# Two of the modulation sections made in each attention are summed by VectorE in two staging tiles, the rest stay matmuls

## The chip, the cores and the metric

The kernel runs on one core of a Trainium2 chip. The metric is the device time of one execution in microseconds (us), here the median of three runs. The engines are TensorE (PE, with its weight loads PEld), VectorE (DVE), ScalarE (ACT), GpSimd (POOL) and SyncE (SP), which issues nearly all DMAs.

## The reference

The program is one inference step of a two-layer backbone. It handles 640 tokens of width 1024: 128 context tokens and 512 latent tokens, two groups that share the weights but not the conditioning vector. Each layer is

```
mod = silu(cond) @ w_mod + b_mod            # 1024 x 9216, split into 9 sections of 1024
sh1, sc1, g1, sh2, sc2, g2, sh3, sc3, g3 = split(mod, 9)
x = LN(alpha*x + 0.5*g1*SwiGLU_1(x*(1+sc1)+sh1))
x = LN(alpha*x + g2*W_out[RG-LRU | GQA | MLA](x*(1+sc2)+sh2))
x = LN(alpha*x + 0.5*g3*SwiGLU_2(x*(1+sc3)+sh3))
```

All is float32. A modulation section (layer, s) is two vectors of 1024 (one for each group's cond), each a product of a vector of 1024 with a 1024x1024 block of `w_mod`, 4 MB. There are 18 sections, numbered s = 0 to 8 in each layer; s = 2, 5 and 8 are gates.

## The kernel before

The big products are split: a float32 weight comes by DMA into a staging tile ("raw", a ring of `NR` = 7 tiles of 128x1024 floats, counted by `raw_out`), ACT rounds it to a high part, DVE subtracts to get the low part, and PE makes three products. The program is a list of steps, each with loads, splits and a body that yields; `run` walks through them, `feed` issues the next loads of one common queue whenever `raw_out` is below `NR`, and `tick` advances background generators once at every yield. A tile scheduler then orders each engine's instructions; nothing in the parts spoken of here is ordered by hand. An instruction can be issued earlier than where it is traced, if its inputs are ready.

A modulation section is eight steps (`mod_steps`), one for each 128 rows of its block of `w_mod`, and can be made in two ways. In `body` a step is four matmuls of 256 columns with `cst`, the two conds as 32 columns of weights, in four column groups of PE (L364); they sum in one bank of the tag `p1`, of which there are two. In `vbody`, used in the FFN stages (`late == "v"`), a step is four DVE operations of 128x512: for each group's cond and each half, raw times one column of `cst` plus the sum so far (L331; the first step has no sum, L329). The two sums are tiles of 128x1024. After the eighth step, eight matmuls with `sel` add up the 128 partitions (L340). Both ways end in `mod_end`: bias, and then a small transpose or a gate's trip through DRAM.

`PLAN` says which sections are made where. In the mixer of layer 0 ("m0") five are made, in that of layer 1 ("m1") three, all with `body`, during the attention. The attention of the latent tokens (`att_sample`) goes through 48 units, one for each pair of a head (8 GQA, then 4 MLA) and a block of 128 queries. A unit is: scores on PE (L1751), the maximum on DVE (L1765) and a tiny product (L1766), the exponent on ACT (L1767), a reciprocal on DVE (L1775), the normalisation on POOL (L1776), five transposes on PE two units later (L1785), their copy on ACT (L1790), and values on PE (L1713), five for each four units. `att_sample` yields twice for each unit, and `env["unit"]` counts units as their scores are traced. Beside it `side` makes the context tokens' attention and MLA's projections.

`mod_fill` is the generator that places the modulation: groups of `MODG` = 4 steps, group i not before unit `MOD0 + i*MODN//len(msteps)` (i counts steps), which is 6, 9, 13, ... 40 in layer 0 and 6, 12, 18, 25, 31, 37 in layer 1, and not before all four raw tiles are traced. The step that starts it, `attend_mods`, comes behind the last projection (`tokens(768, ...)`), which already runs beside the first units. Its loads stand in the queue behind the weights of MLA and ahead of those of `W_out`.

Of the kernel before, what the change touches and what calls it, by code (L numbers as in the profile page):

```python
# [18 lines left out]
P = 128  # L19
D = 1024  # L20
# [18 lines left out]
NB = 23  # L39
LAG = 2  # L40
AVN = (0, 0, 5, 0)
MOD0, MODN, MODG = 6, 38, 4
YK, YQ0, YQ1, YC, YR, YM = 5, 1, 0, 0, 2, 2
NORM_ACT = 256, 512
EVAC = 2, 1
# [15 lines left out]
GROUPS = (1, slice(0, 128)), (0, slice(128, 640))  # L61
PLAN = {
    "f00": [[], [], [(0, 2), (0, 3), (0, 4)]],
    "m0": [[], [(0, 5), (0, 6), (0, 7), (0, 8), (1, 0)]],
    "f01": [[], [], [(1, 1), (1, 2)]],
    "f10": [[], [], [(1, 3), (1, 4)]],
    "m1": [[], [(1, 5), (1, 6), (1, 7)]],
    "f11": [[], [], [(1, 8)]],
}
LN_LAG = 1, 1  # L70
# [39 lines left out]
class Kern:  # L110
# [194 lines left out]
    def mod_steps(self, l, s, late=False):  # L305

        nc, I = self.nc, self.I
        st = {}
        steps = []
        for k in range(KT):  # L310
            hold = {}

            def load(k=k, hold=hold):
                t = self.raw([P, D])
                nc.sync.dma_start(out=t, in_=I["w_mod"][l, k * P : (k + 1) * P, s * D : (s + 1) * D])
                hold["raw"] = t

            def vbody(k=k, hold=hold):

                if k == 0:  # L320
                    st["acc"] = [self.X([P, D]) for _ in range(2)]
                    st["bm"] = bias_rows()
                for g in range(2):
                    acc, c = st["acc"][g], self.cst[:, k, g : g + 1]
                    for h in range(2):
                        cs = slice(h * 512, (h + 1) * 512)
                        e = nc.gpsimd if (g, h) in VP else nc.vector
                        if k == 0:
                            e.tensor_scalar(acc[:, cs], hold["raw"][:, cs], c, 1.0, op0=ALU.mult, op1=ALU.mult)  # L329
                        else:  # L330
                            e.scalar_tensor_tensor(  # L331
                                acc[:, cs], hold["raw"][:, cs], c, acc[:, cs], op0=ALU.mult, op1=ALU.add
                            )
                        yield
                self.raw_out -= 1
                if k == KT - 1:
                    st["ps"] = self.p1()
                    for g in range(2):
                        for c in range(4):
                            nc.tensor.matmul(  # L340
                                st["ps"][32 * c : 32 * c + 32, 0:256],
                                lhsT=self.sel[:, g],
                                rhs=st["acc"][g][:, c * 256 : (c + 1) * 256],
                                start=(g == 0),
                                stop=(g == 1),
                                skip_group_check=True,
                                tile_position=(0, 32 * c),
                            )
                    self.mod_end(l, s, st)

            def bias_rows():
                bm = self.bm[self.bm_i]
                self.bm_i ^= 1
                src = I["b_mod"][l, s * D : (s + 1) * D].rearrange("(c n) -> c n", c=4)
                for g in range(2):
                    nc.sync.dma_start(out=bm[g : 97 + g : 32, :], in_=src)
                return bm

            def body(k=k, hold=hold):
                if k == 0:  # L360
                    st["ps"] = self.p1() if late else self.p2()[:, 0, :]
                    st["bm"] = bias_rows()
                for c in range(4):
                    nc.tensor.matmul(  # L364
                        st["ps"][32 * c : 32 * c + 32, 0:256],
                        lhsT=self.cst[:, k, :],
                        rhs=hold["raw"][:, c * 256 : (c + 1) * 256],
                        start=(k == 0),
                        stop=(k == KT - 1),
                        skip_group_check=True,  # L370
                        tile_position=(0, 32 * c),
                    )
                self.raw_out -= 1
                if k == KT - 1:
                    self.mod_end(l, s, st)
                yield

            steps.append(Step([load], [], vbody if late == "v" else body))
            steps[-1].ready = lambda hold=hold: "raw" in hold
        return steps  # L380

# [770 lines left out]
    def mixer_steps(self, l, mods):  # L1152
        nc, I, O = self.nc, self.I, self.O
        env = {}
# [421 lines left out]
        def mla_weights():  # L1576

            h = [{}, {}]

            def load0():  # L1580
                t = self.raw([P, 2, 384])
                w = I["mla_w_uq"][l]
                nc.sync.dma_start(out=t[:, 0], in_=w[0:128])
                for d in range(2):
                    nc.sync.dma_start(out=t[64 * d : 64 * d + 64, 1], in_=w[128:192])
                h[0]["raw"] = t

            def load1():
                t = self.raw([P, 512])
                nc.sync.dma_start(out=t[:, 0:256], in_=I["mla_w_uk"][l])  # L1590
                nc.sync.dma_start(out=t[:, 256:512], in_=I["mla_w_uv"][l])
                h[1]["raw"] = t

            def sp(i, key, shape):
                def go():
                    env[key] = split(h[i]["raw"], shape)
                    self.raw_out -= 1

                go.ready = lambda: "raw" in h[i]
                return go  # L1600

            def body():
                yield

            return Step([load0, load1], [sp(0, "uq", [P, 2, 384]), sp(1, "ukv", [P, 512])], body)
# [287 lines left out]
        S = []  # L1893

        def proj(c0, post, first=None):
            h = {}
            ld, sp = self.weight(I["w_in"][l][:, c0 : c0 + P].rearrange("(k p) f -> p k f", p=P), [P, KT, P], h, self.W)
            n = len(S)

            def body():  # L1900
                h["ps"] = self.p2("pg" if n % 2 == 0 else "pu")
                for c in range(2):
                    yield from self.mtile(h["ps"], h, c)
                post(h["ps"])
                yield

            return h, ld, sp, body

        def bgpost(gen):
            def post(ps):  # L1910
                self.bg.append(gen(ps))

            return post

        h0, l0, s0, _ = proj(0, None)
        h1, l1, s1, _ = proj(256, None)
# [14 lines left out]
            yield  # L1931

        S.append(Step([l0, l1], s0 + s1, first))
        for ls in mods[0]:
            S += self.mod_steps(*ls, late=True)
        keep = {}

        def xa1(ps):
# [90 lines left out]
        for c0, post in ((128, xa1), (384, ga1)):  # L2029
            h, ld, sp, body = proj(c0, post)  # L2030
# [3 lines left out]
        h, ld, sp, body = proj(1504, bgpost(c_post))  # L2034
# [38 lines left out]
            self.drain()  # L2073

        S.append(mla_weights())
        msteps = [st for ls in mods[1] for st in self.mod_steps(*ls, late=True)]

        def mod_fill():

            for i in range(0, len(msteps), MODG):  # L2080
                part = msteps[i : i + MODG]
                while env.get("unit", 0) < MOD0 + i * MODN // len(msteps) or not all(st.ready() for st in part):
                    yield
                for st in part:
                    for _ in st.body():
                        pass
                yield

        def attend_mods():
            self.bg.append(mod_fill())  # L2090
            yield from attend()
# [364 lines left out]
```

## Time and profile before

| | |
|---|---|
| median of 3 runs | 2520.85 us (2518.51 to 2522.15) |
| the profiled execution | 2519.84 us, of which the span from first to last instruction is 2518.0 us |
| PE, PEld busy | 2418.0 us (96%), 2186.4 us (87%) |
| DVE busy | 1934.2 us (77%) |
| ACT, POOL busy | 1135.9 us (45%), 347.0 us (14%) |

Busy is the share of the span in which an engine has at least one instruction under way. Register, branch and DMA-issuing instructions don't count. The first and the second attention lie at about 608 to 767 us and 1849 to 2000 us of the span. Unit numbers here count from 0, by the reductions of L1765.

### The profile page before, as it was taken

How to read it: one execution, taken by the hardware profiler on the slowest of the kernel's cores; microseconds unless marked ns; L12 is line 12 of the kernel's file. 1: busy time of each engine (PE TensorE's matmuls, PEld its weight loads, DVE VectorE, ACT ScalarE, POOL GpSimd, SP SyncE). 2: the span in 40 equal slices, each digit the busy share in tenths (PEclk: the TensorE clock that was granted, in tenths of full speed). 3: DMA queues.
4: the chain of work that ended last, by engine and by line, in shares of the span. 5: the costliest groups of instructions: out<-in, count | busy, mean ns of one | idle time of the engine just before them, and what ended most of it. 6: DMA issues, size and time to landing. Idle time of an engine off the chain costs nothing. (4 is left out here: it accounts for less than half of the span.)

```text
span 2518.0 us, 40146 instructions
## 1 busy us (share of the span) xinstructions
PE 2418.0 (96%) x15732; PEld 2186.4 (87%) x15732; DVE 1934.2 (77%) x3333; ACT 1135.9 (45%) x2062; POOL 347.0 (14%) x347
## 2 busy tenths in 40 slices
PE   8899999998999999999999999999999999999997
PEld 7898998898769999999889989988976799999986
DVE  5898977878555988876799878778785479777777
ACT  3443343565662543333355333435656534443332
POOL 2100002026322000000100000021363210000022
PEclk9999999999999999999999999999999999999999
DMA  8344433232562343432424333242223423333331
GB/s 283 108 147 142 152 118 109 79 105 65 176 219 85 105 139 118 131 112 84 126 68 149 120 124 116 89 123 87 80 96 123 132 76 102 115 103 105 114 93 51
DMA packets 273270, 293.80 MB, mean 117 GB/s; under 512 B 13645, under 2 KB 224185, under 8 KB 273081
## 3 DMA queue, kind: packets, MB, share of 16 engines
q1 hardware_dynamic: 273080, 291.23, 37.0%
q8 instruction: 124, 2.03, 0.3%
q14 instruction: 66, 0.53, 0.1%
HBM read 270.79 MB, written 18.83 MB: 115 GB/s over the span
## 5 line engine op out<-in xcount | busy, mean ns | idle before, releaser
L930 PE MATMUL pb<-u,w 128*128 128x320 f32 x3600 | 554.6, 309 | 2.2 <-DVE b L976 2.2
L930 PEld LDWEIGHTS pb<-u,w 128*128 128x128 f32 x3600 | 534.8, 188 | 7.0 <-issue 4.6
L930 PE MATMUL pb<-s,w 128*128 128x320 f32 x2700 | 424.4, 310 | 2.0 <-DVE w L906 0.9
L902 ACT CAST w<-raw 128x512 fp32r<-128x512 f32 x525 | 315.9, 619 | 230.6 <-DVE raw L898 151.6
L930 PEld LDWEIGHTS pb<-s,w 128*128 128x128 f32 x2700 | 402.4, 188 | 7.1 <-DVE w L906 1.8
L906 DVE TENSOR_TENSOR w<-raw,w 128x512 fp32r<-128x512 f32 x525 | 357.0, 692 | 45.8 <-ACT w L902 44.4
L1042 PE MATMUL p<-dw,b 128*128 128x512 f32 x830 | 330.3, 398 | 18.8 <-DVE x L1055 16.7
L1043 PE MATMUL p<-dw,b 128*128 128x512 f32 x830 | 324.5, 391 | 0.0
L1044 PE MATMUL p<-dw,b 128*128 128x512 f32 x830 | 324.2, 391 | 0.0
L194 ACT CAST dw<-raw 128x1024 fp32r<-128x1024 f32 x86 | 87.9, 1051 | 367.7 <-PE p L1043 331.0
L1042 PEld LDWEIGHTS p<-dw,b 128*128 128x128 f32 x830 | 156.1, 188 | 68.4 <-DVE x L1055 34.5
L1055 DVE TENSOR_TENSOR x<-x,p 128x512 f32<-128x512 f32 x200 | 136.5, 682 | 86.2 <-PE p L1044 85.6
L1044 PEld LDWEIGHTS p<-dw,b 128*128 128x128 f32 x830 | 156.2, 188 | 33.3
L1043 PEld LDWEIGHTS p<-dw,b 128*128 128x128 f32 x830 | 156.3, 188 | 29.2
L331 DVE SCALAR_TENSOR_TENSOR x<-raw,cst,x 128x512 f32<-128x512 f32 x224 | 163.6, 751 | 19.5 <-DMA raw<-in_w_mod 19.5
L526 PE MATMUL p<-u,w 128*128 128x320 f32 (+2 forms) x528 | 167.1, 318 | 7.4 <-ACT u L517 7.4
L1004 POOL TENSOR_SCALAR x<-x 128x1024 f32<-128x1024 f32 x8 | 9.5, 1184 | 1151.0 <-DMA x<-gd 500.0
L527 PE MATMUL p<-u,w 128*128 128x320 f32 (+2 forms) x528 | 166.4, 317 | 1.5 <-DVE u L518 1.4
L528 PE MATMUL p<-u,w 128*128 128x320 f32 (+2 forms) x528 | 164.8, 314 | 0.0
L199 DVE TENSOR_TENSOR dw<-raw,dw 128x1024 fp32r<-128x1024 f32 x86 | 105.3, 1228 | 41.9 <-ACT dw L194 41.7
L1765 DVE TENSOR_REDUCE sm<-p 128x1 f32<-128x640 f32 x96 | 78.8, 822 | 42.3 <-PE p L1751 37.6
L898 DVE TENSOR_TENSOR raw<-raw,raw 128x512 f32<-128x512 f32 x150 | 103.0, 687 | 10.6 <-DMA raw<-in_ffn_w_up 8.7
(363 smaller groups left out, 4436.1 us busy)
## 6 DMA issues: line engine op xcount, KB each, us to landing
raw<-in_w_mod SPq DMA_DIRECT2D x132, 512.0 KB
raw<-in_ffn_w_gate SPq DMA_DIRECT2D x88, 512.0 KB
raw<-in_ffn_w_up SPq DMA_DIRECT2D x88, 512.0 KB
raw<-in_ffn_w_down SPq DMA_DIRECT2D x88, 512.0 KB
xd<-x SPq DMA_DIRECT2D x30, 512.0 KB
raw<-in_w_in SPq DMA_DIRECT2D x26, 512.0 KB
t<-xd SPq DMA_DIRECT2D x40, 256.0 KB
raw<-in_w_out SPq DMA_DIRECT2D x16, 512.0 KB
```

What stands on the lines that cost most here:

```text
L199: nc.vector.tensor_sub(l, hold["raw"], f(hold["hi"]))
L331: e.scalar_tensor_tensor(acc[:, cs], hold["raw"][:, cs], c, acc[:, cs], op0=ALU.mult, op1=ALU.add)
L526: nc.tensor.matmul(out, lhsT=wh, rhs=xh, start=start, stop=False)
L527: nc.tensor.matmul(out, lhsT=wh, rhs=xl, start=False, stop=False)
L528: nc.tensor.matmul(out, lhsT=wl, rhs=xh, start=False, stop=stop)
L902: nc.scalar.copy(w[:, 0], at(src))
L906: nc.vector.tensor_sub(w[:, 1], at(src), f(w[:, 0]))
L930: nc.tensor.matmul(out, lhsT=a1, rhs=b1, start=(start and k == 0 and i == 0), stop=(k == 3 and i == 2), skip_group_check=not start,)
L1042: nc.tensor.matmul(pt, lhsT=hh[:, ts], rhs=d["hi"][:, cs], start=(i == 0), stop=False)
L1043: nc.tensor.matmul(pt, lhsT=hh[:, ts], rhs=d["lo"][:, cs], start=False, stop=False)
L1044: nc.tensor.matmul(pt, lhsT=hl[:, ts], rhs=d["hi"][:, cs], start=False, stop=(i == len(ms) - 1))
L1055: nc.vector.tensor_add(x[:, cs], x[:, cs], pt)
```

## The change

In each mixer the first two sections of the list, (0,5) and (0,6) in layer 0, (1,5) and (1,6) in layer 1, are made by `vbody`, now also for `late == "ring"`. Their sums are not tiles of the pool `X` but two tiles of the raw ring: two entries `room` ahead of a section's first load take them, and `raw_out -= 2` gives them back at its end. The other sections (three in layer 0, one in layer 1) stay with `body` in groups of four. `mod_fill` goes by a list of turns: vector step i not before unit `3 + i*22//16`, groups of four PE steps not before units 25, 28, 31, 35, 38 and 41 in layer 0 and 25 and 35 in layer 1. A vector step yields after its second and fourth operation and once more, so it takes three ticks, one unit and a half.

```
-MOD0, MODN, MODG = 6, 38, 4
+V0, VN, P0, PN = 3, 22, 25, 20
...
-    "m0": [[], [(0, 5), (0, 6), (0, 7), (0, 8), (1, 0)]],
+    "m0": [[(0, 5), (0, 6)], [(0, 7), (0, 8), (1, 0)]],
...
-    "m1": [[], [(1, 5), (1, 6), (1, 7)]],
+    "m1": [[(1, 5), (1, 6)], [(1, 7)]],
...
-                    st["acc"] = [self.X([P, D]) for _ in range(2)]
+                    if late == "v":
+                        st["acc"] = [self.X([P, D]) for _ in range(2)]
...
+                    if late == "ring":
+                        self.raw_out -= 2
                     self.mod_end(l, s, st)
...
-            steps.append(Step([load], [], vbody if late == "v" else body))
+            def room():
+
+                st.setdefault("acc", []).append(self.raw([P, D]))
+
+            lds = [room, room, load] if late == "ring" and k == 0 else [load]
+            steps.append(Step(lds, [], vbody if late in ("v", "ring") else body))
...
-        for ls in mods[0]:
-            S += self.mod_steps(*ls, late=True)
...
-        msteps = [st for ls in mods[1] for st in self.mod_steps(*ls, late=True)]
+
+        vsteps = [st for ls in mods[0] for st in self.mod_steps(*ls, late="ring")]
+        psteps = [st for ls in mods[1] for st in self.mod_steps(*ls, late=True)]
+        turns = [(V0 + i * VN // len(vsteps), [st]) for i, st in enumerate(vsteps)]
+        turns += [(P0 + i * PN // len(psteps), psteps[i : i + 4]) for i in range(0, len(psteps), 4)]
+        msteps = vsteps + psteps
...
-            for i in range(0, len(msteps), MODG):
-                part = msteps[i : i + MODG]
-                while env.get("unit", 0) < MOD0 + i * MODN // len(msteps) or not all(st.ready() for st in part):
+            for unit, part in turns:
+                while env.get("unit", 0) < unit or not all(st.ready() for st in part):
                     yield
                 for st in part:
-                    for _ in st.body():
-                        pass
+                    for i, _ in enumerate(st.body()):
+                        if part[0] in vsteps and i % 2:
+                            yield
                 yield
```

## Rows read from the trace of the kernel before

**Rows 1.** The page's first part: busy time of the engines over the span.

```profile
PE 2418.0 (96%) x15732; PEld 2186.4 (87%) x15732; DVE 1934.2 (77%) x3333; ACT 1135.9 (45%) x2062; POOL 347.0 (14%) x347
```

**Rows 2.** Busy time by stretches: before unit 3, units 3 to 28, the rest.

```profile
core 0: us, PE busy (x) PEld busy (x) DVE busy (x) ACT busy (x) POOL busy (x), PEclk, DMA share, GB/s
596.80:619.80 23.00, 20.84 (x160) 20.26 (x160) 19.36 (x30) 12.35 (x26) 14.42 (x14) 0.93 0.24 77
619.80:700.50 80.70, 79.37 (x669) 55.48 (x667) 48.33 (x120) 52.41 (x103) 34.91 (x38) 1.00 0.50 175
700.50:767.00 66.50, 62.95 (x484) 45.15 (x483) 35.04 (x87) 45.28 (x85) 17.18 (x22) 1.00 0.65 205
1837.90:1859.90 22.00, 19.22 (x155) 18.24 (x154) 19.21 (x30) 12.08 (x25) 14.29 (x14) 1.00 0.26 80
1859.90:1934.70 74.80, 72.85 (x570) 52.20 (x569) 46.59 (x113) 52.29 (x103) 34.81 (x38) 1.00 0.33 116
1934.70:2000.00 65.30, 61.00 (x460) 45.01 (x460) 35.26 (x91) 45.42 (x85) 17.19 (x22) 1.00 0.52 162
```

**Rows 3.** Groups of instructions by line: busy us, mean ns of one | idle before.

```profile
L331 DVE SCALAR_TENSOR_TENSOR x<-raw,cst,x 128x512 f32<-128x512 f32 x224 | 163.6, 751 | 19.5 <-DMA raw<-in_w_mod 19.5
...
L364 PE MATMUL p<-raw,cst 128*32 128x256 f32 x512 | 41.0, 385 | 1.2 <-ACT u L1624 1.2
L364 PEld LDWEIGHTS p<-raw,cst 128*32 128x32 f32 x512 | 15.5, 109 | 15.6 <-issue 6.9 <-ACT u L1624 1.7 <-DVE sm L1765 0.2
L329 DVE TENSOR_SCALAR x<-raw,cst 128x512 f32<-128x512 f32 x32 | 14.4, 480 | 4.0 <-DMA raw<-in_w_mod 4.0
L340 PE MATMUL p<-x,sel 128*32 128x256 f32 x128 | 8.6, 385 | 0.0
```

**Rows 4.** L364 alone, in the stretches of rows 2.

```profile
619.80:700.50 80.70, 17.22 (x224) 6.86 (x224) 1.00 0.50 175
700.50:767.00 66.50, 8.26 (x96) 2.86 (x96) 1.00 0.65 205
1859.90:1934.70 74.80, 9.99 (x128) 3.90 (x128) 1.00 0.33 116
1934.70:2000.00 65.30, 5.51 (x64) 1.92 (x64) 1.00 0.52 162
```

**Rows 5.** DVE's timeline of units 8 and 9: start us, us.

```profile
643.04 0.81 DVE L1765 TENSOR_REDUCE sm<-p 128x1 f32<-128x640 f32 x1
...
644.85 0.82 DVE L1765 TENSOR_REDUCE sm<-p 128x1 f32<-128x640 f32 x1
645.59 0.15 DVE L1775 RECIPROCAL sm<-sm 128x1 f32<-128x1 f32 x1
```

**Rows 6.** PE's timeline at unit 5.

```profile
628.41 0.64 PE L364 MATMUL p<-raw,cst 128*32 128x256 f32 x8
...
633.09 0.63 PE L364 MATMUL p<-raw,cst 128*32 128x256 f32 x6
```

**Rows 7.** DVE's timeline in the first FFN stage.

```profile
122.22 0.87 DVE L329 TENSOR_SCALAR x<-raw,cst 128x512 f32<-128x512 f32 x2
...
130.20 2.07 DVE L331 SCALAR_TENSOR_TENSOR x<-raw,cst,x 128x512 f32<-128x512 f32 x3
```

**Rows 8.** The timeline around a POOL operation in an FFN stage.

```profile
274.10 0.68 DVE L906 TENSOR_TENSOR w<-raw,w 128x512 fp32r<-128x512 f32 x1
...
274.33 1.35 POOL L1004 TENSOR_SCALAR x<-x 128x1024 f32<-128x1024 f32 x1 [202.89 <-DVE mv L402]
...
274.69 1.53 DVE L331 SCALAR_TENSOR_TENSOR x<-raw,cst,x 128x512 f32<-128x512 f32 x1
```

**Rows 9.** The timeline around one normalisation in the attention.

```profile
693.92 0.16 DVE L447 SCALAR_TENSOR_TENSOR bp<-mv,vec 128x8 f32<-128x8 f32 x1
693.96 0.81 POOL L1776 TENSOR_SCALAR b<-b,sm 128x640 f32<-128x640 f32 x1 [0.58 <-DVE sm L1775]
...
694.12 0.67 DVE L448 TENSOR_TENSOR bp<-bp,mv 128x16 f32<-128x16 f32 x1
```

**Rows 10.** L1776 alone, in units 3 to 28: us, POOL busy (x).

```profile
619.80:700.50 80.70, 21.42 (x26) 1.00 0.50 175
1859.90:1934.70 74.80, 21.33 (x26) 1.00 0.33 116
```

**Rows 11.** SP's timeline before and in the first units.

```profile
575.23 5.02 SPq L315 DMA_DIRECT2D raw<-in_w_mod  x3
...
596.84 19.69 SPq L315 DMA_DIRECT2D raw<-in_w_mod  x3
```

**Rows 12.** Busy time by stretches of 10 us, columns as in rows 2.

```profile
570.00:580.00 10.00, 5.97 (x37) 5.43 (x36) 9.93 (x9) 4.27 (x6) 5.08 (x4) 0.83 0.27 67
```

## The prediction

> **What bounds the kernel now.** I read the page's totals first: PE is busy for 96% of the span and DVE for 77% [rows 1], so over the whole kernel PE sets the time and DVE seems to have room. The change touches only the two attentions, so the totals decide nothing; I cut each attention where the new gates cut it. Since `mod_fill` is started only behind the last projection, at about unit 4, and sixteen vector steps of three ticks fill 24 units, the vector work is traced between units 4 and 28. The view by stretches is therefore cut at the reductions of units 3 and 28 [rows 2]. In that stretch (80.7 us in layer 0, 74.8 in layer 1) PE is busy for 98% and 97%, DVE for 60% and 62%. Behind it PE is at 95% and 93%, DVE at 53% and 54%. Just ahead of it DVE is at 84% and 87%. So today's first stretch goes at PE's pace with 32.4 and 28.2 us of idle DVE, and that idle time is what the change wants to use.
>
> **What is removed from PE.** 512 records of L364 stand for 64 steps (two records for each of four matmuls), busy 41.0 us [rows 3]: 0.64 us a step. 32 of the 64 steps go: 20.5 us. Four sections now end with the `sel` product instead: 128 records took 8.6 us for eight sections, so 1.07 us each, 4.3 us for four. PE is relieved of 16.2 us net.
>
> **What is added to DVE.** Each section is 4 operations of L329 and 28 of L331, medians 480 and 751 ns as recorded [rows 3]. The recorded end of one overlaps the start of the next: three of L331 in a row take 2.07 us and two of L329 take 0.87 [rows 7], so the steps between starts are (2.07-0.75)/2 = 0.66 and 0.87-0.48 = 0.39 us. A section is 4*0.39+28*0.66 = 20.1 us, the two of a layer 40.3 us (by recorded durations 45.9).
>
> **Does it fit between units 4 and 28?** DVE is already busy there for 48.3 us in layer 0 and 46.6 in layer 1 [rows 2]. With the new work it is 88.6 of 80.7 us, and 86.9 of 74.8. It doesn't fit: DVE would be the bound of this stretch in both layers, whatever PE is spared.
>
> Can work leave the stretch? Not to the back: a vector operation is traced between units that wait for DVE too, and is older than the reductions behind it. To the front, yes: pieces of the PE group gated by unit 9 (scores of unit 8) ran at 628.4 to 633.7 [rows 6], 9 us before the reduction of unit 8 at 643.0 [rows 5], so ready work does go ahead of its place. But just ahead of the stretch DVE has only 3.6 and 2.8 us idle [rows 2], and the loads limit it too: three raw tiles come free at 575 us and three more from 597 us [rows 11], and now the first two are taken by sums. I credit all of that idle time, 3.6 and 2.8 us.
>
> The ring of seven is five tiles for loads while a section is summed. A vector step takes about one and a half units, some 5 us, so five tiles cover 25 us, more than any load needs; L331 waited for its data for 19.5 us in 224 operations [rows 3], and on a DVE with a backlog other work fills that. I cost the ring at nothing. If that cover fails, it is 19.5/224*128 = 11 us at most over both layers.
>
> **POOL and DVE exclude each other.** A POOL operation began while DVE ran L906, and the next DVE operation, L331, took 1.53 us instead of 0.75 [rows 8]. In the attention the tiny L448, which has two inputs in SBUF, took 0.67 us and ended with the normalisation that ran at that time [rows 9]; its like took 0.16. The reductions and most of today's DVE work there read PSUM or one input, and meet little of this; the 128 new operations all do. There are 26 normalisations in the stretch, 21.4 us in all [rows 10]. If each stops DVE for its whole length, the price is 21.4 us a layer; if a reduction or another unaffected operation is always next in DVE's queue, nothing. About half of DVE's time in the new stretch is new operations, so I take half: 10.7 us. What queues behind a stopped vector operation is the next unit's reduction, and behind that its exponent, its normalisation and PE's transposes.
>
> **The sum for units 3 to 28.** Layer 0: 48.3+40.3-3.6+10.7 = 95.7 us against 80.7, +15.0. Layer 1: 46.6+40.3-2.8+10.7 = 94.8 against 74.8, +20.0. PE's own work there falls to about 79.4-17.2+2.1 = 64 us and 72.9-10.0+2.1 = 65 us [rows 2, 4], so PE stands idle for a third and its relief is worth nothing.
>
> **Units 28 to 47.** PE sets the pace here. Layer 0 has 96 records, 12 steps, in this stretch [rows 4]; now all 24 PE steps lie in it: 12*0.64 = 7.7 us more. In layer 1 it has 64 records, 8 steps, and keeps 8: 0. The loads for `W_out` follow the last PE group, which is gated at 41 instead of 40 in layer 0 and 35 instead of 37 in layer 1; I cost that at nothing, because behind the attention `W_out`'s first products find PE busy with the last values.
>
> The other edits cost nothing: `mod_end` is the same, and the `p1` bank that a PE section holds for its whole length is now held only at the end in the first stretch, which helps nobody there since DVE is the bound.
>
> **Total.** 15.0+20.0+7.7 = 42.7 us on the profiled execution's 2519.84 us: 2562.5 us. The median shown is 1 us above that execution, which I ignore.
>
> **A rule that would change the gain.** In the first stretch PE is busy for 98% but its weight loads for 55.5 of 80.7 us, 69% [rows 2]. The Trainium skill (Perfetto Trace Analysis, Identifying the Most-Contended Engine) says that matmul busy time is a poor measure of how near PE is to its limit, because matmuls are pipelined, and that the share of weight loading should be read instead. By that rule PE has a third of headroom today and sparing it would be worth at most the weight loads removed, 15.5/2 = 7.8 us [rows 3], not 16.2; DVE, whose occupancy the page calls a fair measure, is then the nearer limit. The sum above stands either way, since it uses PE's relief at nothing.
>
> **Both ends.** Low: no exclusion, and each of the 120 (113) DVE operations hides 0.08 us of its recorded end in the next, as the reduction of unit 9 did (0.82 recorded, 0.74 to the next start) [rows 5]: 9.6 and 9.0 us. Then layer 0 gives 48.3-9.6+40.3-3.6-80.7 = -5.3, layer 1 46.6-9.0+40.3-2.8-74.8 = +0.3, and of the 7.7 us behind, 3.5 vanish in PE's idle time there (66.5-63.0) [rows 2]: 4.2. Together -0.8: 2519. High: full exclusion, recorded durations, nothing ahead: 48.3+45.9+21.4-80.7 = +34.9, 46.6+45.9+21.4-74.8 = +39.1, +7.7: 2601.5.
>
> **Rivals.**
> Faster, PE's relief counts: the vector operations only fill gaps and spread over the whole attention, where DVE is idle for 32.4+31.5 us in layer 0 and 28.2+30.0 in layer 1 [rows 2], more than 40.3. Then the time falls by the 16.2 us of PE: 2504 us. For it: work does run ahead of its place [rows 6]. Against: the gates and the order of tracing put all of it before unit 28. It decides if 15 us (layer 0) and 20 us (layer 1) of the 40.3, that is a third to a half, leave the stretch. By the rule above this gain would be near 8 us. Chance 0.12.
> Even: DVE packs without a gap, and the exclusion hides behind reductions; that is the low end, 2515 to 2525 us. Against: the chain of a unit goes back and forth between DVE, ACT and POOL, which leaves gaps even where DVE is the busiest. Chance 0.09.
> Much slower: the high end, 2601 us and more: full exclusion, and POOL waiting for DVE in turn, so that the normalisations come late and the units' chains stretch. PE's clock could also fall: in the 10 us where PE was busy for 60% the granted clock was 0.83 of full, so it spent a part of them at 1.2 GHz instead of 2.4 [rows 12]. But 65 us of PE work at 0.83 are 78, still below DVE's 95, so the clock alone adds nothing. Chance 0.09.
> My forecast, DVE-bound between units 4 and 28, has the other 0.70.
>
> **Range and chances.** 2520 to 2602 us leaves out the faster rival, half of the even one and the part above 2602: 0.12+0.04+0.04. Within 0.2% is 5 us, about what a measurement of this kernel can tell from no change. Faster by more 0.12, within it 0.09, slower by more 0.79.
>
> **What would show it.** In the profile after: between the reductions of units 3 and 28, DVE at 95% or more and PE at 65 to 75%, with a length of some 95 us in both layers; L331 352 times, with a mean above 0.80 us; L1776 with a mean above today's 0.82 us; L364 256 times. Behind unit 28, layer 0 longer by 4 to 8 us and layer 1 unchanged; the FFN stages unchanged. I am wrong if DVE has idle time left between units 3 and 28, if vector operations lie well before 590 us or behind unit 30, or if L331 keeps its 0.75 us beside the normalisations.

## The result, and the profile after

| | median us | lowest to highest | runs |
|---|---|---|---|
| before | 2519.68 | 2517.80 to 2522.15 | 4 |
| after | 2561.68 | 2559.01 to 2563.62 | 4 |

The change makes the kernel slower: ratio 1.0161, 95% interval 1.0149 to 1.0173. The profiled execution took 2563.62 us against 2519.84 before, 43.8 us more; forecast were 42.7.

In the new kernel the lines stand a little lower: L331 is L332, L329 L330, L364 L367, L1751 L1759, L1765 L1773, L1767 L1775, L1775 L1783, L1776 L1784, L1785 L1793, L1790 L1798.

The page's first part, to be read beside [rows 1]:

```profile
PE 2426.3 (95%) x15540; PEld 2189.6 (85%) x15540; DVE 2016.2 (79%) x3461; ACT 1136.1 (44%) x2062; POOL 363.6 (14%) x347
```

DVE is busy for 82 us more. PE has 192 instructions fewer and is yet busy for 8 us longer, so these totals say little about what was saved.

Busy time by stretches, cut at the same reductions as [rows 2] (unit 3, unit 28, and behind the last unit):

```profile
core 0: us, PE busy (x) PEld busy (x) DVE busy (x) ACT busy (x) POOL busy (x), PEclk, DMA share, GB/s
600.40:623.40 23.00, 17.50 (x131) 15.43 (x129) 22.66 (x37) 10.81 (x22) 12.97 (x12) 1.00 0.05 17
623.40:716.10 92.70, 76.75 (x476) 55.80 (x477) 81.81 (x167) 51.76 (x101) 40.49 (x39) 0.89 0.31 89
716.10:793.40 77.30, 71.86 (x582) 49.07 (x580) 37.28 (x97) 46.72 (x87) 18.00 (x23) 0.98 0.75 265
1862.00:1886.00 24.00, 18.51 (x139) 16.45 (x137) 23.66 (x38) 10.81 (x22) 14.04 (x12) 1.00 0.08 24
1886.00:1975.20 89.20, 72.94 (x476) 52.24 (x477) 81.63 (x167) 51.77 (x101) 40.83 (x39) 0.94 0.31 92
1975.20:2041.70 66.50, 62.44 (x464) 46.94 (x463) 35.21 (x94) 46.33 (x87) 18.04 (x23) 0.97 0.56 182
```

Units 3 to 28 are where most of it went: 92.7 us instead of 80.7 and 89.2 instead of 74.8. DVE's busy time there rose from 48.3 and 46.6 us to 81.8 and 81.6, and PE's share fell from 98% and 97% to 83% and 82%. But DVE isn't full over the whole stretch either: it is idle for 10.9 and 7.6 us. Cut further, at units 8, 13 and 18, the stretch shows where (layer 0, then layer 1, columns as above):

```profile
623.40:651.30 27.90, 23.40 (x118) 17.51 (x119) 22.08 (x42) 16.35 (x32) 17.78 (x18) 0.82 0.26 76
651.30:668.10 16.80, 13.76 (x101) 11.72 (x99) 16.05 (x36) 9.41 (x18) 6.83 (x8) 0.91 0.22 63
668.10:685.00 16.90, 14.27 (x91) 10.02 (x91) 13.73 (x31) 8.74 (x18) 4.68 (x5) 0.79 0.38 107
685.00:716.10 31.10, 25.32 (x173) 16.55 (x172) 29.96 (x61) 17.27 (x34) 11.20 (x10) 1.00 0.36 104
1886.00:1912.90 26.90, 22.21 (x119) 16.15 (x120) 22.22 (x43) 16.46 (x32) 17.70 (x18) 0.87 0.26 79
1912.90:1929.60 16.70, 13.66 (x101) 11.63 (x100) 15.95 (x36) 9.41 (x18) 6.92 (x8) 0.95 0.21 64
1929.60:1944.10 14.50, 11.75 (x90) 7.92 (x89) 13.47 (x31) 8.62 (x18) 5.00 (x5) 0.94 0.44 124
1944.10:1975.20 31.10, 25.31 (x173) 16.55 (x172) 29.99 (x61) 17.27 (x34) 11.20 (x10) 1.00 0.35 103
```

In units 8 to 13 and 18 to 28 DVE is busy for 95% and 96% in both layers, and these parts are equally long in both. The idle time lies in units 3 to 8 (5.8 and 4.7 us) and 13 to 18 (3.2 and 1.0 us), where the granted clock is lowest. Before, the four parts took 23.2, 13.7, 12.5 and 31.2 us in layer 0 and 23.2, 12.0, 13.2 and 26.5 in layer 1. The lengths of the parts, from reduction to reduction (the third part ends here at the reduction of unit 47, not behind it):

| us | last scan of the mixer to unit 0 | units 0 to 3 | 3 to 28 | 28 to 47 |
|---|---|---|---|---|
| before, layer 0 | 23.0 | 11.6 | 80.7 | 60.5 |
| after, layer 0 | 24.8 | 12.0 | 92.7 | 71.3 |
| before, layer 1 | 22.6 | 11.1 | 74.8 | 58.3 |
| after, layer 1 | 24.9 | 12.0 | 89.2 | 59.5 |

Layer 0 grows by 1.8+0.4+12.0+10.8 = 25.0 us, layer 1 by 2.3+0.9+14.4+1.2 = 18.8: 43.8 together. The rest nets to nothing: the execution was 1.3 us later before the first attention, 3.5 us came back between unit 47 and the second mixer's last scan, and 2.2 went behind the second attention. I did not trace these three.

The groups of DVE, POOL and PE that the prediction named:

```profile
L332 DVE SCALAR_TENSOR_TENSOR x<-raw,cst,x 128x512 f32<-128x512 f32 x224 | 163.6, 751 | 20.2 <-DMA raw<-in_w_mod 20.0
...
L332 DVE SCALAR_TENSOR_TENSOR raw<-raw,cst,raw 128x512 f32<-128x512 f32 x112 | 91.6, 831 | 0.1
...
L1784 POOL TENSOR_SCALAR b<-b,sm 128x640 f32<-128x640 f32 x96 | 91.0, 948 | 196.5 <-DVE sm L1783 132.6 <-DVE sm L1774 34.2 <-PE p L1759 13.0
...
L367 PE MATMUL p<-raw,cst 128*32 128x256 f32 x256 | 20.0, 386 | 0.3 <-DMA raw<-in_w_mod 0.3
```

The 112 new operations (the ones that sum into raw) take 831 ns where those of the FFN stages take 751, and they waited for data for 0.1 us in all. The ring of five was hardly a cost here: what remains is 1.8 us in which, by the profile, DVE's L330 waited for a `sel` product (L341), which reads the tiles of the sums. Half of the 512 matmul records are gone.

DVE's timeline (start us, us) ahead of unit 0, whose reduction is at 611.42, and at 682 us:

```profile
605.02 0.87 DVE L330 TENSOR_SCALAR raw<-raw,cst 128x512 f32<-128x512 f32 x2
605.81 0.74 DVE L332 SCALAR_TENSOR_TENSOR raw<-raw,cst,raw 128x512 f32<-128x512 f32 x1
...
608.17 1.51 DVE L332 SCALAR_TENSOR_TENSOR raw<-raw,cst,raw 128x512 f32<-128x512 f32 x2
...
611.42 0.83 DVE L1773 TENSOR_REDUCE sm<-p 128x1 f32<-128x640 f32 x1
...
682.33 0.82 DVE L1773 TENSOR_REDUCE sm<-p 128x1 f32<-128x640 f32 x1
683.07 0.15 DVE L1783 RECIPROCAL sm<-sm 128x1 f32<-128x1 f32 x1
683.14 0.73 DVE L332 SCALAR_TENSOR_TENSOR raw<-raw,cst,raw 128x512 f32<-128x512 f32 x1
683.79 0.15 DVE L1774 TENSOR_TENSOR sm<-sm,rsq 128x1 f32<-128x1 f32 x1
683.86 1.22 DVE L332 SCALAR_TENSOR_TENSOR raw<-raw,cst,raw 128x512 f32<-128x512 f32 x1
```

Five operations of the first section already run ahead of unit 0. At 682 us DVE is back to back: the tiny reciprocal and product of a unit stand between the new operations, and one of these takes 1.22 us where the one before took 0.73. The same length shows in the timeline of both engines at 671 us, where a normalisation was under way when the operation began:

```profile
671.55 1.15 POOL L1784 TENSOR_SCALAR b<-b,sm 128x640 f32<-128x640 f32 x1 [2.68 <-PE p L1759]
...
672.02 1.22 DVE L332 SCALAR_TENSOR_TENSOR raw<-raw,cst,raw 128x512 f32<-128x512 f32 x1
```

And what PE waited for in units 3 to 28 of layer 0 (us in total, times, longest). Before, this view had two rows there, 0.6 us and 0.5 us.

```profile
PE p L1759 <- ACT u L1798: 7.0, 9, 0.8
PE p L1793 <- ACT u L1798: 2.7, 3, 2.2
PE p L1793 <- DVE b L1436: 2.2, 1, 2.2
```

The scores wait for the copies of the transposes, ACT's L1798: a chain that goes through DVE, ACT, POOL and PE now comes late, at a place that names neither DVE nor the new operations.

### The profile page after: what moved, and what is told of

Read it like the earlier page. It is cut to its first block, busy times and chain, and to the rows that moved or that the text cites. A ratio compares the mean times of both kernels' runs of the same rounds, so it can differ in the third digit from the quotient of the medians.

```text
span 2561.9 us, 39873 instructions
## 1 busy us (share of the span) xinstructions
PE 2426.3 (95%) x15540; PEld 2189.6 (85%) x15540; DVE 2016.2 (79%) x3461; ACT 1136.1 (44%) x2062; POOL 363.6 (14%) x347
## 5 line engine op out<-in xcount | busy, mean ns | idle before, releaser
L1063 DVE TENSOR_TENSOR x<-x,p 128x512 f32<-128x512 f32 x200 | 136.4, 682 | 83.8 <-PE p L1052 83.1
L332 DVE SCALAR_TENSOR_TENSOR x<-raw,cst,x 128x512 f32<-128x512 f32 x224 | 163.6, 751 | 20.2 <-DMA raw<-in_w_mod 20.0
L1784 POOL TENSOR_SCALAR b<-b,sm 128x640 f32<-128x640 f32 x96 | 91.0, 948 | 196.5 <-DVE sm L1783 132.6
L1759 PE MATMUL p<-x,b 128*128 128x320 f32 (+1 forms) x448 | 96.9, 343 | 20.4 <-ACT u L1798 17.0
```

Of the source, the lines that this page charges most:

```text
L332: e.scalar_tensor_tensor(acc[:, cs], hold["raw"][:, cs], c, acc[:, cs], op0=ALU.mult, op1=ALU.add)
L1063: nc.vector.tensor_add(x[:, cs], x[:, cs], pt)
```

## The experiments

Every kernel was timed beside the kernel before on the same chip; differences are between those medians.

**1. How much vector work, and does the exclusion count?** The theory of the prediction: DVE's work and what POOL takes from it set the length. The rival: it is the presence of the steps (ring, loads, order), whatever their size. `few_ops` leaves the sums out of all but a section's first step, 8 operations an attention instead of 64; `half_ops` leaves the sums of one cond out, 36. Loads, ring and turns stay.

```
 cs = slice(h * 512, (h + 1) * 512)
 ...
+if late == "ring" and k:                 # half_ops: "and k and g"
+    yield
+    continue
 if k == 0:
```

> The changed kernel without the 28 of 32 vector operations of each ring section that belong to its steps 1 to 7; only the four of step 0 stay. Loads, ring, gates, yields and the sel products stay. It leaves out seven eighths of those four sections' sums. Theory (VectorE's added work is what costs): the first stretch falls back to TensorE's pace without the removed matmuls, about 80.7-17.2+2.1 = 66 us in layer 0 and 74.8-10.0+2.1 = 67 us in layer 1, the second stretch of layer 0 stays 8 to 11 us longer than before; 2500 to 2512 us in all. Rival (the ring of five tiles, the gates and the later matmuls cost, whatever VectorE does): 2550 us or more.

> As few_ops, but only the second group's sum is left out behind step 0: 14 of the 28 operations of each ring section stay out. Theory (VectorE is full): its content in the first stretch is then about 48.3+21.8-3.6+5 = 72 us in layer 0 and 71 us in layer 1, below or near today's 80.7 and 74.8, so most of the loss is gone: 2515 to 2527 us. Rival (each vector operation delays the units' chain by its own length wherever it stands, full or not): the time lies in the middle between few_ops and the changed kernel, about 2533 us.

The other two leave the normalisation (POOL's L1784) out of all 96 units, in the kernel after and in the kernel before.

```
-    nc.gpsimd.tensor_scalar(pt, pt, st[:, 2:3], 1.0, ...)
```

> The changed kernel without the 96 normalisations of the latent attention on GpSimd (the exponents go unnormalised into the transposes). To be compared with before_no_norm. Theory (the exclusion of GpSimd and VectorE is worth 10.7 us a layer): the difference between the two falls from 42 us to about 21 us. Rival (the exclusion is hidden behind reductions): it stays at 38 to 42 us.

> The kernel before without the same 96 normalisations. TensorE is busy for 98% of the first stretch, so little is gained: 2505 to 2518 us by the theory that TensorE sets the pace there. If the units' chain sets it, the 0.8 us of each normalisation show in part: below 2500 us.

| | median us | before | ratio | 3 to 28, layers 0 and 1 | 28 to 47 |
|---|---|---|---|---|---|
| few_ops | 2530.84 | 2523.64 | 1.0032 [1.0020, 1.0044] | 76.4, 75.4 | 70.2, 61.0 |
| half_ops | 2533.69 | 2523.64 | 1.0046 [1.0031, 1.0060] | 77.0, 78.2 | 68.5, 58.2 |
| after_no_norm | 2562.95 | 2523.64 | 1.0153 [1.0130, 1.0176] | 88.8, 90.9 | 73.4, 57.5 |
| before_no_norm | 2523.20 | 2523.64 | 1.0004 [0.9990, 1.0019] | 80.9, 74.9 | 59.9, 59.2 |

The stretches of `few_ops` and of `half_ops`, layer 0 ahead of layer 1, columns as above:

```profile
622.60:698.90 76.30, 69.50 (x472) 51.55 (x471) 47.01 (x112) 52.56 (x103) 34.78 (x38) 0.96 0.10 27
1868.20:1943.60 75.40, 68.48 (x472) 50.27 (x472) 46.43 (x112) 52.52 (x103) 34.77 (x38) 0.98 0.10 27
```

```profile
622.90:700.00 77.10, 69.06 (x476) 50.30 (x477) 61.97 (x139) 52.11 (x101) 39.13 (x39) 0.98 0.33 95
1869.10:1947.30 78.20, 70.17 (x476) 51.66 (x477) 61.94 (x138) 52.03 (x101) 38.78 (x39) 0.96 0.33 94
```

With DVE at 47 of 76 us (62%) and at 62 of 77 (80%) the stretch is about equally long in layer 0 and 2.8 us apart in layer 1; with 82 us it is 15.7 and 11.0 longer again. The first half of the vector work fits and the second doesn't. With loads, ring and turns the same in all three, the amount of vector work at these gates is shown to be the cost of this stretch, and the rival falls. From `half_ops` to the kernel after, 7.7 and 7.5 us of that lie in units 8 to 13 and 18 to 28, where DVE is full; the other 8.0 and 3.5 lie in units 3 to 8 and 13 to 18, where DVE has idle time and the granted clock is lowest. Of the 42.0 us of the change, 7.2 are there with hardly any vector work: they lie in units 28 to 47 and in the start.

Both expectations of `few_ops` missed. The 2500 to 2512 us asked that the stretch fall to PE's remaining work, 66 and 67 us. It stayed at 76.4 and 75.4, with PE busy for 69.5 and 68.5: in layer 0 PE does 9.9 us less than before [rows 2] and 4.3 come back, in layer 1 4.4 less and nothing comes back. `half_ops` missed its 2515 to 2527 as well. It lies at the figure of its rival, 2533, but not in the middle between `few_ops` and the kernel after, where the rival had put it and which is 2548 beside this kernel before.

The exclusion is real, but it isn't in the bill. Without normalisations the new operations fall from 831 to 772 ns:

```profile
L332 DVE SCALAR_TENSOR_TENSOR raw<-raw,cst,raw 128x512 f32<-128x512 f32 x112 | 84.8, 772 | 0.1
```

That is (831-772)*56 = 3.3 us an attention. The difference between the two kernels without it is 2562.95-2523.20 = 39.8 us, as good as the 42.0 with it, where the forecast's 10.7 a layer asked for some 21. And PE's longest wait in units 3 to 28 of layer 0 is the same to the digit, 7.0 us in 9 times:

```profile
PE p L1759 <- ACT u L1797: 7.0, 9, 0.8
```

`before_no_norm` gained nothing, where 2505 to 2518 us had been expected. So leaving POOL's step out of a unit's chain shortens neither kernel.

**2. Is it the order or the place?** `p_beside` moves the PE groups back beside the vector steps: gates by the formula of the kernel before (6, 12, ... 37 in layer 0, 6 and 25 in layer 1), by a second generator, with the loads in the order of the gates. If units 28 to 47 of layer 0 pay for PE groups that were pushed there, they come back to some 60 us. `spread` also spreads the gates of the vector steps over units 3 to 42, `one_section` does that with one vector section instead of two, and `few_ops_p_beside` joins `few_ops` and `p_beside`, so that PE is spared its steps and DVE has hardly more to do. In `spread` and `one_section` (and in `spread_softmax_first` below) more sections are under way at once than the two bias tiles are meant for, so that a section can get another's bias; the work is the same.

```
-V0, VN, P0, PN = 3, 22, 25, 20
+V0, VN, P0, PN = 3, 22, 6, 38            # spread, one_section: 3, 42, 6, 38
...
+vturns = [(V0 + i * VN // len(vsteps), [st]) for i, st in enumerate(vsteps)]
+pturns = [(P0 + i * PN // len(psteps), psteps[i : i + 4]) for i in range(0, len(psteps), 4)]
+msteps = [st for _, part in sorted(vturns + pturns, key=lambda t: t[0]) for st in part]
...
-def mod_fill():
+def mod_fill(turns):
...
-self.bg.append(mod_fill())
+self.bg.append(mod_fill(vturns))
+self.bg.append(mod_fill(pturns))
```

> The changed kernel with the two kinds of steps in two generators: vector steps as now (units 3 to 25), groups of matmul steps beside them at units 6 to 44 instead of behind them at 25 to 45, loads in the order of the gates. Theory (units 28 to 47 of layer 0 are longer because 12 more matmul steps lie there): that stretch goes back from 71 to about 61 to 64 us, units 3 to 28 stay, since TensorE has room there: 2551 to 2556 us. Rival (units 28 to 47 are longer as a backlog of the first stretch): no change, 2560 us or more.

> As p_beside, with the vector steps gated over units 3 to 45 instead of 3 to 25. Same work. Theory (what costs is VectorE full in the first stretch): half of the operations leave it and find 30 us of idle VectorE behind unit 28; units 3 to 28 fall to about 77 us as in half_ops, units 28 to 47 to about 60 to 63: 2522 to 2532 us. Rival (the operations cost their place in VectorE's order wherever they stand): 2545 us or more.

> As spread, but only one section in each attention is made by VectorE, the others by matmuls in groups of four at units 6 to 44. Theory: 20 us of vector work over 48 units hides, and TensorE is spared 8 steps in each attention, of which only those count that lie where TensorE is the limit: 2514 to 2522 us, at best a little faster than the kernel before. Rival (any vector operation among the units delays their chains): 2528 us or more.

> few_ops with the gates of p_beside: it leaves out seven eighths of the sums of the ring sections, and the matmul steps are spread as in the kernel before, only fewer. It measures what sparing TensorE 16 steps in each attention is worth when nothing is put on VectorE. If TensorE sets the pace of the attention: 16.2 us less than before, about 2507 us. If the chains of the units set it and the matmuls only fill gaps: 2516 us or more.

| | median us | before | ratio | 3 to 28, layers 0 and 1 | 28 to 47 |
|---|---|---|---|---|---|
| p_beside | 2557.55 | 2521.71 | 1.0146 [1.0126, 1.0167] | 93.5, 100.7 | 58.8, 54.6 |
| spread | 2535.71 | 2521.71 | 1.0051 [1.0035, 1.0067] | 84.4, 83.8 | 59.3, 60.9 |
| one_section | 2540.49 | 2521.71 | 1.0081 [1.0065, 1.0097] | 86.3, 87.0 | 66.3, 57.9 |
| few_ops_p_beside | 2520.53 | 2521.71 | 0.9993 [0.9984, 1.0003] | 79.8, 78.2 | 59.6, 56.5 |

The stretches 3 to 28 of `p_beside`:

```profile
619.40:712.90 93.50, 82.65 (x606) 54.21 (x607) 84.67 (x172) 50.99 (x99) 40.14 (x38) 0.98 0.55 179
...
1868.80:1969.50 100.70, 84.27 (x550) 57.47 (x550) 85.69 (x172) 53.96 (x102) 40.41 (x38) 0.90 0.41 131
```

Three readings. First, units 28 to 47 of layer 0 came back from 71.3 to 58.8 us at once, and units 3 to 28 of layer 0 took on 130 more instructions of PE (606 against 476) for 0.8 us: the pushed groups cost the 10.8 us there, and in this layer's stretch, which DVE holds up, PE's work is nearly free. Second, layer 1 gave much of that gain back: 100.7 us instead of 89.2, against 4.9 us won in its units 28 to 47. Of the 7.2 us between its two layers 5.5 lie in units 13 to 18: 19.8 us with a granted clock of 0.74 against 14.3 with 1.00, for the same 12 vector operations. Over the whole stretch the clock was 0.90, a part of it at 1.2 GHz, but it was 0.89 in the 92.7 us of layer 0 after, so the clock alone doesn't make the length. What else does, I haven't settled. So `p_beside` missed its 2551 to 2556 us, by 1.6. (Its profiled execution took 2551.80 us, 5.8 below its median, so the two stretches may understate it.)

Third, `few_ops_p_beside` is the test of the rival "PE's relief counts". PE is spared half of its steps, DVE does 8 operations an attention, and the time is that of before, 1.2 us apart. Net, the relief is worth about nothing, as forecast; from the last scan to unit 3 this kernel loses 1.9 us over both layers, so a gain of that size may be hidden.

`spread` is better than after by some 28 us. Its vector operations ran ahead of their gates, the last in unit 38 of layer 0 and 36 of layer 1, and only 18 and 15 of the 64 lay behind unit 28, where half had been expected. With 2535.71 us it missed its 2522 to 2532, and it is still slower than before. `one_section` misses what the amount of work would give, 2514 to 2522 us: with 32 vector operations an attention it should lie near `half_ops` (36), and its stretch is 9 us longer in both layers. Its PE groups run beside them, which costs `few_ops_p_beside` 3 us against `few_ops`, and they are one section more than there, 34 more records in this stretch; some 6 us an attention, less what that section costs, stay unexplained. They lie in units 3 to 8 of layer 0 and 8 to 16 of layer 1. Its time lies where its rival had put it, 2528 us or more: that any vector operation among the units delays their chains isn't excluded for vector work beside PE groups.

**3. Do the softmax operations come late because they queue behind vector operations?** The rival to "too much work": each reduction and reciprocal stands behind a few vector operations, as in the timeline above, and with the right order DVE's idle time would take the work. Here the scheduler is told to put a unit's maximum, product and reciprocal 200 places further ahead than they are traced, in the kernel after, in `spread` and in the kernel before.

```
+with self.tc.high_priority(offset=SUMS):
     nc.vector.tensor_reduce(st[:, 0:1], v, axis=AX.XY, op=ALU.max, negate=True)
     nc.vector.tensor_mul(st[:, 3:4], st[:, 0:1], fa)
...
+with self.tc.high_priority(offset=SUMS):
     nc.vector.reciprocal(st[:, 2:3], st[:, 1:2])
```

> The changed kernel, in which the scheduler is told to put each unit's maximum, tiny product and reciprocal 200 places further ahead than they are traced, so that a vector operation of a modulation section that is ready at the same time comes behind them. Same work, same gates. Theory (VectorE's amount of work between units 3 and 28 is the limit): units 3 to 28 stay within 5 us of 92.7 and 89.2 us, in all 2552 us or more. Rival (the vector operations cost because they stand ahead of the units' short operations): most of the loss goes, 2525 to 2545 us.

> The kernel spread with the three operations put ahead. As in spread, a bias tile can be loaded for a later section before an earlier one has read it, so some sections get a wrong bias; the work is the same. Theory: the vector operations can now fall back into the idle VectorE behind unit 28, units 3 to 28 come near 77 us: 2522 to 2530 us. Rival (order and placement cost as such): as spread, about 2535 us.

> The control: the kernel before with the same three operations put ahead. There they compete with side work alone: 2512 to 2524 us by both.

The last one takes matmuls out of the kernel before: the steps 1 to 6 of each section made in the attentions have none.

```
-for c in range(4):
+for c in range(4) if not late or k in (0, KT - 1) else ():
```

> The kernel before with only the first and the last step's matmuls of each section made in the attentions: it leaves out 48 of the 64 steps' products, 30.7 us of busy TensorE. If TensorE's busy share of 97% in the attentions is a limit: about 2490 us. If those matmuls fill gaps that the units' chains leave anyway: 2505 us or more.

| | median us | before | ratio | 3 to 28, layers 0 and 1 | 28 to 47 |
|---|---|---|---|---|---|
| softmax_first | 2561.55 | 2514.70 | 1.0187 [1.0167, 1.0206] | 90.1, 90.1 | 72.5, 63.0 |
| spread_softmax_first | 2533.14 | 2514.70 | 1.0076 [1.0056, 1.0097] | 83.9, 84.8 | 63.5, 61.8 |
| before_softmax_first | 2520.36 | 2514.70 | 1.0029 [1.0016, 1.0042] | 82.0, 77.2 | 60.3, 58.4 |
| before_few_matmuls | 2506.37 | 2514.70 | 0.9964 [0.9955, 0.9974] | 74.5, 82.2 | 57.3, 56.8 |

The stretches of `softmax_first`:

```profile
622.30:712.40 90.10, 73.58 (x464) 54.28 (x466) 81.68 (x165) 52.00 (x101) 43.99 (x39) 0.91 0.28 91
1881.70:1971.90 90.20, 73.61 (x464) 54.27 (x466) 81.69 (x166) 52.05 (x102) 43.99 (x39) 0.91 0.28 90
```

The order isn't it. The stretches move by -2.6 and +0.9 us with DVE's busy time the same, and in all three kernels the ratio to before is no better than without the edit. So `spread_softmax_first` missed its 2522 to 2530 us and lies where its rival had put it, near `spread`. `before_few_matmuls` removes 48 of 64 steps, 48*0.64 = 30.7 us of PE's busy time by [rows 3], and gives 8.3 us: about a quarter of that busy time comes back, in attentions whose first stretches read 98% and 97% busy for PE. It isn't a clean price: layer 1's stretch got longer, 82.2 us, and in 35 us of it PE was less busy and the granted clock was 0.80, so that what was left ran slower:

```profile
1855.00:1890.00 35.00, 27.99 (x167) 21.91 (x166) 20.88 (x45) 19.48 (x36) 13.17 (x14) 0.80 0.26 86
```

No kernel of the study beats the kernel before by doing the change otherwise; `few_ops_p_beside` equals it, but leaves the sums out.

## Why the prediction was right

It forecast 2562.5 us and a loss; 2561.68 was measured. By its steps:

- **DVE doesn't fit between units 4 and 28: right, and shown** by the three amounts of experiment 1.
- **"Today's first stretch goes at PE's pace": wrong as far as it was tested.** `few_ops` took 9.9 and 4.4 us of PE's busy time out of it and 4.3 and nothing came back. The sum didn't hang on it.
- **The sum for units 3 to 28**: 95.7 and 94.8 us forecast, 92.7 and 89.2 measured; +15.0 and +20.0 against +12.0 and +14.4. Its parts were worse than their sum. The exclusion stood at 10.7 us a layer; the new operations' mean shows 3.3, and taking the normalisations away gave nothing that could be measured. Against that DVE's idle time stood at zero, and DVE was busy for 88% and 92% where I had named 95% or more as the sign, and idle time on DVE was one of my signs of being wrong: 10.9 and 7.6 us of it. The argument against the even rival, that a unit's chain goes back and forth between the engines and leaves gaps, stood beside the sum and not in it, and it isn't shown: with the same chain DVE is busy for 96% of units 18 to 28, and taking POOL out of the chain moved the stretch by -3.9 and +1.7 us. The gaps lie in units 3 to 8, where DVE was idle for 6.4 us before as well, and in units 13 to 18.
- **PE's work there, 64 and 65 us, and PE at 65 to 75%**: wrong, 76.8 and 72.9 us, 83% and 82%. The granted clock fell to 0.89 and 0.94 against 1.00 [rows 2], so a part of PE's work ran at 1.2 GHz. I had named such a fall and held that the clock alone adds nothing. Units 13 to 18 speak against that: with the same 12 new operations and DVE busy for 13.7 and 13.5 us, they took 16.9 us in layer 0 at a clock of 0.79 and 14.5 in layer 1 at 0.94, and PE's busy time differs as much, 14.3 and 11.8. In both layers PE had stood idle for 2.2 us just before, waiting for one of ACT's copies; then the clock was at 1.2 GHz from 665.1 to 675.3 us in layer 0 and from 1928.0 to 1931.4 in layer 1. This difference and that of units 3 to 8 are the whole 3.5 us between the layers' stretches; no run holds the clock still, so it is read and not tested.
- **PE's relief is worth nothing: right, and shown** by `few_ops_p_beside` (1.2 us). By the Trainium skill (Perfetto Trace Analysis, Identifying the Most-Contended Engine) matmul busy time is not a good measure of how near PE is to its limit; `before_few_matmuls` agrees, with 8.3 us for 30.7 us of it. The faster rival fell on this: even spread out, the change lost 14.0 us.
- **Units 28 to 47**: layer 0 +7.7 forecast, +10.8 measured; layer 1 0 and +1.2. The cause is shown by `p_beside`, which brought 71.3 back to 58.8. 192 records lie there, 15.1 us, against 96 and 8.3 us before [rows 4], as counted; the price was 3.9 us more than these 6.9 us of busy time. The granted clock was 0.98 there against 1.00; that part isn't explained further.
- **Missing: the start.** Nine vector operations a layer, 6.0+0.9 us of DVE, ran ahead of unit 3, in a stretch with 3.6 and 2.8 us of idle [rows 2]. I credited the idle time as a gain and did not ask what the rest would push: from the last scan to unit 3 it takes 2.2 us longer in layer 0 and 3.2 in layer 1, and DVE is full there, 22.66 of 23.00 us. `few_ops` and `half_ops` pay for it too (2.2 and 2.5 us in layer 0) with 8 and 10 operations there; `one_section`, with 4, does not (-0.1 us).
- **The ring of five at nothing: right for after** (0.1 us of waiting for data, 1.8 us for the tiles of the sums).
- **Slips in the working**: a section of vector work comes to 20.0 us by its own terms, not 20.1; the 480 and 751 ns are means and not medians; and of the 128 new operations 112 are of the form of L331, so that L332 stands 336 times and not 352. Its mean is 831 ns for these and the old 751 for the 224 of the FFN stages; the 16 of L330 kept their 0.48 us.

So the mechanism held in the units where DVE is full, 8 to 13 and 18 to 28; in the others the loss came with idle DVE and a slower PE, which the sum didn't have, and the good total is in part luck. Against the forecast, in us over both layers: exclusion -14.8 (3.3 instead of 10.7, twice); DVE's other work in the stretch -12.3 (81.8-3.3 = 78.5 instead of 85.0, and 81.6-3.3 = 78.3 instead of 84.1; more operations ran ahead than were credited); idle time of DVE +18.5; start +5.4; units 28 to 47 +4.3. Together +1.1.

## What to carry to other kernels

Before work is moved to an engine with idle time, add it to that engine's busy time in the very stretch where the gates will put it: here the first 20 us fitted in 30 us of idle and the second 20 did not. Cut that stretch further: in layer 0 a mean of 88% was 95 and 96% in the units where DVE set the pace and 79 and 81% in the others. Price what is taken from the other engine by what comes back when it is simply left out (8.3 us of 30.7 here), not by its busy time. And ask of each step that is moved what it pushes: the PE groups pushed behind unit 28 cost more than their own length, and work that ran ahead of its place pushed the start.

## What the runs showed that I had not expected

- Of the 26 new vector operations that began while a normalisation ran on POOL, 16 took 0.88 to 1.29 us instead of 0.74, and every one of these ended 0.54 us behind the end of the normalisation; the other ten kept their length, eight of them having begun in its last 0.07 us. The normalisations grow too, from 814 to 948 ns in the mean; and yet the kernels with and without normalisations differ by the same 40 us.
- The granted clock can be 0.90 in a stretch where PE is busy for 84% (`p_beside`, layer 1) and 0.98 in one with 88% (layer 0), with lengths of 100.7 and 93.5 us. Which of the two is cause is open, beyond what units 13 to 18 show above.
- One vector section (`one_section`, +18.8 us) cost more than two spread over the same gates (`spread`, +14.0); the intervals of the two ratios just touch. Open as well: no run told the loads, the ring of raw tiles and the PE groups apart there.
